# Expert weights in pieces of 2 contraction tiles by 1024 columns, with a PSUM pair for the gate and one for the up projection

## The chip, the cores and the metric

One core of one Trainium2 chip runs the whole program in one launch. The metric is the time of an execution on the device in microseconds (us); several executions are timed and the median counts. All inputs and the output lie in the chip's HBM. The engines named below are TensorE (PE; its weight loads are a row of their own, PEld), VectorE (DVE), ScalarE (ACT), GpSimd (POOL) and SyncE (SP), whose queue issues the loads of the weights.

## The reference, cut to what matters

A decoder trunk of two layers works on 256 tokens of 1024 float32 channels. Each layer has a mixer; then comes a dense SwiGLU on the first layer, and on the second layer a SwiGLU with 8 experts, two of them for each token. The change touches the experts alone:

```python
def moe_swiglu(h, router_w, w1, w3, w2):          # t: [256, 1024]
    logits = jnp.einsum('td,de->te', t, router_w)
    top_vals, top_idx = lax.top_k(logits, TOP_K)  # 2 of 8
    ...
    for e in range(N_EXPERTS):
        a = t @ w1[e]                             # w1, w3: [1024, 2816]
        b = t @ w3[e]
        out = out + gates[:, e:e + 1] * ((jax.nn.silu(a) * b) @ w2[e])   # w2: [2816, 1024]
```

All of it is float32, and the products must be about as exact as float32.

## The kernel before, in words

**Weights.** All weights are streamed once, in loads of 1 MB (`wload`, lines 72 to 89). SP issues the load of a raw tile; ACT then rounds it into a part `whi` (line 86), and DVE subtracts to get the rest, `wlo` (line 88). Each product of the reference becomes three matmuls on such parts: high by high, high by low and low by high. Four raw buffers (more at times: `ring` lends some), three `whi` buffers and two or three `wlo` buffers make up the stream, and the three engines work it off one load after the other.

**Experts.** `moe` gathers each expert's tokens into 128 slots, so that a matmul has 128 rows of slots and up to 512 columns of weights. `slots` then runs over the experts `e` and over pieces of the hidden width of 2816 (`FCH`: five pieces of 512 columns and one of 256). For a piece, `up_proj` multiplies by w1, and again by w3, into the two banks of one PSUM tile `ab` (tag `mm`, two tiles deep). Then ACT takes the Silu of the first bank (line 976) and DVE multiplies by the second (line 977), which gives `sae`. During the next piece `turn` transposes `sae` on PE (line 890) and splits it into `ahe` and `ale`, and `down` multiplies these by w2 into the two PSUM tiles `ye` of the expert, one for each half of the model's width (lines 906 to 908). A piece of 512 takes two loads of w1, two of w3 and two of w2; the last piece takes one of each.

**Scatter.** When an expert is complete, `gated` scales `ye` by the token's gate and splits it into two parts (ACT line 933, DVE line 934): into `tokA` for an even expert, into four tiles `y` of 512 columns for an odd one. Those four lie in buffers lent by the activations' tags, `st01` and `st02` for the first half of the width, `st00` and `st10` for the second. After an odd expert, PE scatters the two experts' rows back to the tokens (`psc`, line 925, PSUM tag `s`, two tiles deep), and DVE adds the result to the residual stream `xt` (line 927). This happens after experts 1, 3 and 5, while the next expert's first piece is under way, and after expert 7, where the final norm and the output follow.

**Order.** A scheduler turns the program into one fixed sequence of instructions for each engine before the run. An engine works its sequence in order; an instruction whose operands or buffers are not free holds up all that stand behind it on that engine.

Of the kernel before, what the change touches and what calls it, by code (L numbers as in the profile page):

```python
# [21 lines left out]
NL = 2            # layers  # L22
# [5 lines left out]
FCH = [(c, min(512, FF - c)) for c in range(0, FF, 512)]  # L28


@with_exitstack
def trunk_kernel(ctx: ExitStack, tc: tile.TileContext, x, w_in, lower_bounds, hgrn_norm_w, conv_w,
# [39 lines left out]
    def wload(src2d, k0, nk, c0, ncol):  # L72
        """rows k0*128.. (nk tiles) x columns c0..c0+ncol, split -> hi, lo [128, nk, ncol]"""
# [100 lines left out]
    # mean squares of the rows of the residual stream, by halves of the width  # L174
# [45 lines left out]
    # ---- the residual stream times a norm's weight, as columns in parts, by halves of the width. The  # L220
    # norm's factor of a token is applied to what is made of them: rstd by token, rbc as a row for all. ----
# [35 lines left out]
    def bounds():  # L257
        """lower bounds of the forget gates: cumulated softmax over the layers, less the first"""
# [33 lines left out]
    # within a block of 4, s <= t  # L292
# [6 lines left out]
    # s in the first, t in the second half of a block of 2m; t of the second halves only  # L299
# [85 lines left out]
    # o = S^T v, normalised per head, gated; token-major  # L385
# [89 lines left out]
    def route_slots(t):  # L475
        """1 + slot of the token within each expert, 0 where not chosen"""
# [6 lines left out]
    # ================= mixer =================  # L483
    def mixer(l):
# [13 lines left out]
        # forget gate, key, query: [key, head, t] in two groups of four heads  # L498
# [21 lines left out]
        # scores, transposed: [s, head, t]  # L520
# [12 lines left out]
        # output gate, token-major: silu(g) * norm weight  # L533
# [10 lines left out]
        # merge gates  # L544
# [12 lines left out]
        # short convolution: [channel, t]  # L557
# [30 lines left out]
        # projections and merge: [d, t]  # L588
# [21 lines left out]
        for g in range(2):  # L610
# [20 lines left out]
            # a token tile after the other, the routing of the first beside the second  # L631
# [25 lines left out]
    # ================= dense SwiGLU =================  # L657
    def dense(l):
# [10 lines left out]
        def down(c0, n, ah, al, w, dh, cs):  # L669
            """columns cs of the weights w, to the half dh of the width"""  # L670
# [11 lines left out]
        for ci, (c0, n) in enumerate(FCH):  # L682
# [15 lines left out]
            else:  # L698
                # the last two: one half of the width after the other
# [22 lines left out]
    # ================= final norm =================  # L722
# [12 lines left out]
    # ================= top-2 expert SwiGLU =================  # L735
    def moe(l):
# [8 lines left out]
        # the factors of a row: of its normalisation, and its gates; by token and by slot  # L745
# [11 lines left out]
        def make_gates():  # L757
            """softmax over the two kept logits"""
# [17 lines left out]
        def late():  # L776
            """what only the scatter needs: the gates, and the largest number of tokens of an expert"""
# [8 lines left out]
        def slots(base):  # L786
            """all experts on their slots base .. base+127"""
# [23 lines left out]
            def gather(e2, first=False):  # L811
# [3 lines left out]
                # one-hot products of the parts: exact  # L815
# [16 lines left out]
                if first:  # L832
                    # the first token tile ahead of the routing of the second
# [40 lines left out]
            def up_proj(src, c0, n, o, xh, xl, es):  # L874
                nh = (KT * n + 2047) // 2048
                per = KT // nh
                for half in range(nh):
                    wh, wl = wload(src, half * per, per, c0, n)
                    for k in range(per):
                        kt = half * per + k  # L880
                        nc.tensor.matmul(o, xh[:, kt, es], wh[:, k, :], start=kt == 0, stop=False)  # L881
                        nc.tensor.matmul(o, xh[:, kt, es], wl[:, k, :], start=False, stop=False)  # L882
                        nc.tensor.matmul(o, xl[:, kt, es], wh[:, k, :], start=False, stop=kt == KT - 1)  # L883

            def turn(e, c0, n, ci, sa, ys):
                """gated activations [slot, f] -> their parts [f, slot]"""
# [4 lines left out]
                ah = big.tile([128, nt, 128], F32R, tag=f"st{ci % 2}1", name="ahe")  # L891
                al = big.tile([128, nt, 128], F32R, tag=f"st{ci % 2}2", name="ale")
# [3 lines left out]
            def down(e, c0, n, ah, al, ys, PT, halves=(0, 1)):  # L896
                nt = n // 128
                for d0, dn in ([(h * 512, 512) for h in halves] if n == 512 else [(0, 1024)]):
                    wh, wl = wload(expert_w2[j, e], c0 // 128, nt, d0, dn)
                    for dh in range(dn // 512):  # L900
                        for k in range(nt):
                            o = ys[d0 // 512 + dh]
                            ds_ = slice(dh * 512, dh * 512 + 512)
                            first = c0 == 0 and k == 0
                            end = c0 + n == FF and k == nt - 1
                            nc.tensor.matmul(o, ah[:, k, :], wh[:, k, ds_], start=first, stop=False)  # L906
                            nc.tensor.matmul(o, ah[:, k, :], wl[:, k, ds_], start=False, stop=False)  # L907
                            nc.tensor.matmul(o, al[:, k, :], wh[:, k, ds_], start=False, stop=end)  # L908
# [27 lines left out]
            pend = None  # L936
# [8 lines left out]
            for e in range(NE):  # L945
# [4 lines left out]
                for ci, (c0, n) in enumerate(FCH):  # L950
# [3 lines left out]
                    ab = psum.tile([128, 2, 512], F32, tag="mm", name="ab")  # L954
                    up_proj(expert_w1[j, e], c0, n, ab[:, 0, 0:n], xh, xl, es)
# [6 lines left out]
                    if base == 0 and e == 0 and ci == 4:  # L962
                        less("tokA")
                    if e == 0 and ci == 3:
                        less("v")
                        PT = hot_t()
                    if pend is not None:
                        pend = turn(*pend)
                    up_proj(expert_w3[j, e], c0, n, ab[:, 1, 0:n], xh, xl, es)
                    if e % 2 == 1 and e + 1 < NE and ci == 2:  # L970
                        less("fc", "qq")
                        nxt = gather(e // 2 + 1)
                    if pend is not None and not final:
                        down(*pend, PT)
                    sa = big.tile([128, n], F32, tag=f"st{ci % 2}0", name="sae")
# [52 lines left out]
```

## Time and profile before

| | before |
|---|---|
| median of 3 runs | 1619.73 us (1618.6 to 1619.83) |
| span of the profiled execution, first to last instruction | 1618.9 us |
| around the span, against the median | 0.8 us |
| mean granted TensorE clock | 0.994 |
| busy: PE, PEld, DVE, ACT | 99%, 88%, 77%, 58% |
| loads of expert weights | 264 of 1 MB, 6.8 us each from issue to landing |

The profile comes from one execution. Its times are in us from the first instruction on; the experts take the stretch from about 827 to 1608. A share of busy time says little by itself: what counts is what an engine waited for when it did not work. The granted clock of TensorE is 1.0 (2.4 GHz) or 0.5 (1.2 GHz).

### The profile page before, as it was taken

The page shows a single profiled execution, that of the slowest core. Times are in us where ns is not written, and L with a number is a line of the kernel's source. Part 1 is how long each engine was busy: PE and PEld are TensorE (multiplying, and loading weights), DVE is VectorE, ACT ScalarE, POOL GpSimd, SP SyncE. Part 2 cuts the span into 40 slices and gives each one's busy share as a digit, 9 for nine tenths or more (in the row PEclk, how much of TensorE's full clock was granted, in tenths as well). Part 3 has the DMA queues.
Part 4 walks back from the last instruction along what each step waited for, and adds up shares of the span by engine and source line. Part 5 has one row for each costly group of instructions (what it writes and reads, how often), then busy time and mean ns, then how long its engine had stood idle before and what let it go on. Part 6 is the DMA issues. An engine that isn't in the chain of part 4 may idle for free.

```text
span 1618.9 us, 23572 instructions
## 1 busy us (share of the span) xinstructions
PE 1594.9 (99%) x9858; PEld 1427.5 (88%) x9858; DVE 1243.7 (77%) x1182; ACT 938.4 (58%) x836; POOL 33.9 (2%) x51
## 2 busy tenths in 40 slices
PE   7999999999999999999999999999999999999997
PEld 7989999999999989999988888888888888888886
DVE  6964785655446965677678898888888888888886
ACT  6434343544335444334467777677776777767775
POOL 2000020000000000010000000000000000000000
PEclk9999999999999999999999999999999999999998
DMA  7544445555654554458568999999999999999992
GB/s 276 183 158 164 149 132 187 180 182 181 201 189 162 177 182 156 157 195 286 171 221 311 352 324 331 337 366 373 339 356 331 364 374 346 365 334 365 373 376 97
DMA packets 215939, 417.06 MB, mean 258 GB/s; under 512 B 6528, under 2 KB 25056, under 8 KB 215824
## 3 DMA queue, kind: packets, MB, share of 16 engines
q1 hardware_dynamic: 215408, 414.25, 73.1%
q8 instruction: 79, 1.29, 0.3%
q0 software_dynamic: 384, 1.21, 0.2%
q14 instruction: 36, 0.29, 0.0%
q10 hardware_dynamic: 32, 0.01, 0.0%
HBM read 414.40 MB, written 1.05 MB: 257 GB/s over the span
## 4 chain that ended last, share of the span: by engine, by line
PE 96%; DVE 2%; ACT 1%; DMA 1%; issue 0%; POOL 0%; SPq 0%; POOLq 0%; DVEq 0%
PE psb L128 11%; PE psb L130 11%; PE psb L132 11%; PE ab L882 10%; PE ab L883 10%; PE ab L881 9%; PE ye L908 5%; PE ye L906 5%; PE ye L907 5%; PE psa L149 2%; PE psa L151 2%; PE psa L150 2%; PE psl L365 1%; PE y L677 1%; PE y L678 1%; PE y L679 1%
## 5 line engine op out<-in xcount | busy, mean ns | idle before, releaser
L86 ACT ACTIVATE whi<-wraw 128x2048 fp32r<-128x2048 f32 (+1 forms) x456 | 760.5, 1679 | 507.8 <-PE psb L130 257.6
L88 DVE TENSOR_TENSOR wlo<-wraw,whi 128x2048 fp32r<-128x2048 f32 (+1 forms) x456 | 900.1, 1993 | 199.7 <-ACT whi L86 93.1
L128 PE MATMUL psb<-hlA,whi 128*128 128x256 f32 x1376 | 393.2, 286 | 2.7 <-ACT hlA L217 2.7
L130 PE MATMUL psb<-hlB,whi 128*128 128x256 f32 x1376 | 390.5, 284 | 0.5 <-DVE hlB L218 0.5
L132 PE MATMUL psb<-hlA,wlo 128*128 128x256 f32 x1376 | 390.3, 284 | 0.0
L128 PEld LDWEIGHTS psb<-hlA,whi 128*128 128x128 f32 x1376 | 264.4, 192 | 3.9 <-ACT hlA L217 3.1
L130 PEld LDWEIGHTS psb<-hlB,whi 128*128 128x128 f32 x1376 | 264.6, 192 | 1.1 <-DVE hlB L218 0.7
L132 PEld LDWEIGHTS psb<-hlA,wlo 128*128 128x128 f32 x1376 | 264.5, 192 | 0.2
L882 PE MATMUL ab<-wlo,bu 128*128 128x512 f32 (+1 forms) x384 | 144.2, 375 | 1.2 <-DVE wlo L88 1.2
L882 PE MATMUL ab<-wlo,fc 128*128 128x512 f32 (+1 forms) x384 | 144.5, 376 | 0.8 <-DVE wlo L88 0.8
L881 PE MATMUL ab<-whi,bu 128*128 128x512 f32 (+1 forms) x384 | 144.2, 376 | 0.0
L881 PE MATMUL ab<-whi,fc 128*128 128x512 f32 (+1 forms) x384 | 143.8, 374 | 0.0
L883 PE MATMUL ab<-whi,kk 128*128 128x512 f32 (+1 forms) x384 | 143.0, 372 | 0.0
L883 PE MATMUL ab<-whi,qq 128*128 128x512 f32 (+1 forms) x384 | 142.9, 372 | 0.0
L907 PE MATMUL ye<-wlo,ahe 128*128 128x512 f32 x352 | 137.7, 391 | 0.7 <-DVE wlo L88 0.7
L908 PE MATMUL ye<-whi,ale 128*128 128x512 f32 x352 | 136.9, 390 | 0.2
L906 PE MATMUL ye<-whi,ahe 128*128 128x512 f32 x352 | 136.6, 390 | 0.0
L882 PEld LDWEIGHTS ab<-wlo,bu 128*128 128x128 f32 x384 | 72.4, 189 | 14.4 <-DVE wlo L88 2.8
L882 PEld LDWEIGHTS ab<-wlo,fc 128*128 128x128 f32 x384 | 72.3, 188 | 14.4 <-DVE wlo L88 2.7
L881 PEld LDWEIGHTS ab<-whi,fc 128*128 128x128 f32 x384 | 72.3, 188 | 12.6
L881 PEld LDWEIGHTS ab<-whi,bu 128*128 128x128 f32 x384 | 72.3, 188 | 12.3
L883 PEld LDWEIGHTS ab<-whi,kk 128*128 128x128 f32 x384 | 72.4, 188 | 12.1
(243 smaller groups left out, 1867.1 us busy)
## 6 DMA issues: line engine op xcount, KB each, us to landing
wraw<-in_expert_w_dram SPq DMA_DIRECT2D x264, 1024.0 KB, 6.8
wraw<-in_w_in_dram SPq DMA_DIRECT2D x72, 1024.0 KB, 5.0
wraw<-in_dense_w_dram SPq DMA_DIRECT2D x33, 1024.0 KB, 5.0
wraw<-in_w_proj_conv_dram SPq DMA_DIRECT2D x8, 1024.0 KB, 5.0
wraw<-in_w_proj_hgrn_dram SPq DMA_DIRECT2D x8, 1024.0 KB, 5.0
wraw<-in_w_out_dram SPq DMA_DIRECT2D x8, 1024.0 KB, 5.0
xt<-in_x_dram SPq DMA_DIRECT2D x2, 512.0 KB, 4.7
out_dram<-bu SPq DMA_DIRECT2D x4, 256.0 KB, 2.9
```

The costliest lines, as they stand in the source:

```text
L86: nc.scalar.activation(hf[:, ks], rf[:, ks], AF.Copy)
L88: nc.vector.tensor_tensor(lf[:, ks], rf[:, ks], hf[:, ks].bitcast(F32), op=ALU.subtract)
L128: nc.tensor.matmul(o, wh[:, k, cs], hh[:, kt, :], start=first, stop=False, skip_group_check=True)
L130: nc.tensor.matmul(o, wh[:, k, cs], hl[:, kt, :], start=False, stop=False, skip_group_check=True)
L132: nc.tensor.matmul(o, wl[:, k, cs], hh[:, kt, :], start=False, stop=last, skip_group_check=True)
L149: nc.tensor.matmul(o, hh[:, kt, ts], wh[:, k, :], start=kt == 0, stop=False)
L881: nc.tensor.matmul(o, xh[:, kt, es], wh[:, k, :], start=kt == 0, stop=False)
L882: nc.tensor.matmul(o, xh[:, kt, es], wl[:, k, :], start=False, stop=False)
L883: nc.tensor.matmul(o, xl[:, kt, es], wh[:, k, :], start=False, stop=kt == KT - 1)
L906: nc.tensor.matmul(o, ah[:, k, :], wh[:, k, ds_], start=first, stop=False)
L907: nc.tensor.matmul(o, ah[:, k, :], wl[:, k, ds_], start=False, stop=False)
L908: nc.tensor.matmul(o, al[:, k, :], wh[:, k, ds_], start=False, stop=end)
```

## The change

The pieces of the experts' hidden width become 1024, 1024 and 768 columns wide (`WIDE`). A load of w1 or w3 then takes 2 contraction tiles of 128 rows by 1024 columns instead of 4 by 512, so that a row of the load is 4096 bytes long instead of 2048 (3072 in the last piece, whose loads have 0.75 MB). A load of w2 takes 2 tiles by the whole width of 1024 instead of 4 by 512. An expert has 35 loads instead of 33, of the same bytes in all. The gate projection gets a PSUM tile `pa` of two banks and the up projection another, `pb`; both come from the tag `mm`, which still has two tiles. Silu, product, transposes and splits work on halves of 512 (or 256) columns as before, now two halves in a row. The matmuls are the same in number and shape.

```diff
+WIDE = [(c, min(1024, FF - c)) for c in range(0, FF, 1024)]
...
             def up_proj(src, c0, n, o, xh, xl, es):
-                nh = (KT * n + 2047) // 2048
-                per = KT // nh
-                for half in range(nh):
-                    wh, wl = wload(src, half * per, per, c0, n)
-                    for k in range(per):
-                        kt = half * per + k
-                        nc.tensor.matmul(o, xh[:, kt, es], wh[:, k, :], start=kt == 0, stop=False)
...
+                for part in range(KT // 2):
+                    wh, wl = wload(src, part * 2, 2, c0, n)
+                    for k in range(2):
+                        kt = part * 2 + k
+                        for p in range(0, n, 512):
+                            ps_ = slice(p, min(p + 512, n))
+                            op = o[:, p // 512, 0:ps_.stop - p]
+                            nc.tensor.matmul(op, xh[:, kt, es], wh[:, k, ps_], start=kt == 0, stop=False)
...
+            def activate(e, c0, n, p, pa, pb):
+                m = min(512, n - p * 512)
+                sa = big.tile([128, m], F32, tag=f"st{p}0", name="sae")
+                nc.scalar.activation(sa, pa[:, p, 0:m], AF.Silu, scale=sc[:, e, 0:1])
+                nc.vector.scalar_tensor_tensor(sa, pb[:, p, 0:m], sc[:, e, 0:1], sa, op0=ALU.mult, op1=ALU.mult)
+                return e, c0 + p * 512, m, p, sa
...
-            def down(e, c0, n, ah, al, ys, PT, halves=(0, 1)):
-                nt = n // 128
-                for d0, dn in ([(h * 512, 512) for h in halves] if n == 512 else [(0, 1024)]):
-                    wh, wl = wload(expert_w2[j, e], c0 // 128, nt, d0, dn)
-                    for dh in range(dn // 512):
-                        for k in range(nt):
-                            o = ys[d0 // 512 + dh]
...
+            def down(e, c0, n, ah, al, ys, PT):
+                for k0 in range(0, n // 128, 2):
+                    wh, wl = wload(expert_w2[j, e], c0 // 128 + k0, 2, 0, 1024)
+                    for k in range(2):
+                        for dh in range(2):
+                            o = ys[dh]
...
-                for ci, (c0, n) in enumerate(FCH):
+                for ci, (c0, n) in enumerate(WIDE):
...
-                    ab = psum.tile([128, 2, 512], F32, tag="mm", name="ab")
-                    up_proj(expert_w1[j, e], c0, n, ab[:, 0, 0:n], xh, xl, es)
+                    pa = psum.tile([128, 2, 512], F32, tag="mm", name="ab")
+                    up_proj(expert_w1[j, e], c0, n, pa, xh, xl, es)
...
+                    pend = [turn(*x) for x in pend]
+                    pb = psum.tile([128, 2, 512], F32, tag="mm", name="ab")
+                    up_proj(expert_w3[j, e], c0, n, pb, xh, xl, es)
...
+                    def acts():
+                        return [activate(e, c0, n, p, pa, pb) + (ys,) for p in range((n + 511) // 512)]
+
+                    if not final:
+                        for x in pend:
+                            down(*x, PT)
+                        pend = acts()
+                        continue
```

`gated` and the scatter are as before, with the same tags for `y`. A second block of the program, for experts with more than 128 tokens, changes alike and is not executed with these inputs. The comments of the file go out, so that lines have other numbers.

The scheduler's order shows what this moves. The number behind a name is that of the tile. The first place is the scatter after expert 1, while the first piece of expert 2 is under way. On PE before, from the last matmul of expert 1's down projection (`ye`) on; `ab_9461` is the next piece of expert 2, with both of its projections:

```order
L908 MATMUL ye_8570<-whi_9410,ale_9369 128x512
L925 MATMUL psc_9430<-tokA_8669,v_8224 128x512 x2
L925 MATMUL psc_9430<-y_9426,v_8224 128x512
L925 MATMUL psc_9436<-tokA_8669,v_8224 128x512 x2
L925 MATMUL psc_9436<-y_9426,v_8224 128x512
L881 MATMUL ab_9461<-whi_9464,fc_8880 128x512
L882 MATMUL ab_9461<-wlo_9465,fc_8880 128x512
L883 MATMUL ab_9461<-whi_9464,qq_8881 128x512
L881 MATMUL ab_9461<-whi_9464,fc_8880 128x512
L882 MATMUL ab_9461<-wlo_9465,fc_8880 128x512
L925 MATMUL psc_9430<-y_9427,v_8224 128x512
L925 MATMUL psc_9436<-y_9427,v_8224 128x512
```

And now, at the same place; `ab_9561` is the gate projection `pa` of the next piece, and takes the buffer of `ab_9307`, the `pa` of the piece before it:

```order
L917 MATMUL ye_8537<-whi_9507,ale_9393 128x512
L934 MATMUL psc_9527<-y_9523,v_8094 128x512
L934 MATMUL psc_9533<-y_9523,v_8094 128x512
L934 MATMUL psc_9527<-y_9524,v_8094 128x512
L934 MATMUL psc_9533<-y_9524,v_8094 128x512
L934 MATMUL psc_9543<-tokA_8754,v_8094 128x512 x2
L934 MATMUL psc_9543<-y_9539,v_8094 128x512
L934 MATMUL psc_9549<-tokA_8754,v_8094 128x512 x2
L934 MATMUL psc_9549<-y_9539,v_8094 128x512
L934 MATMUL psc_9543<-y_9540,v_8094 128x512
L934 MATMUL psc_9549<-y_9540,v_8094 128x512
L883 MATMUL ab_9561<-whi_9564,fc_8929 128x512
```

Before, matmuls of the next piece stand between those of the scatter; now twelve of the scatter stand in one block (two of them are a row with x2), and the next piece's first matmul is behind all of them.

The second place is the same moment on ACT, and then on DVE. On ACT before:

```order
L86 ACTIVATE whi_9464<-wraw_9462 128x2048
L86 ACTIVATE whi_9482<-wraw_9480 128x2048
L933 ACTIVATE y_9426<-ye_8569,sc_7740 128x512
L933 ACTIVATE y_9442<-ye_8570,sc_7740 128x512
L86 ACTIVATE whi_9509<-wraw_9507 128x2048
L976 ACTIVATE sae_9458<-ab_9328,sc_7740 128x512
```

On ACT now:

```order
L942 ACTIVATE y_9523<-ye_8536,sc_7740 128x512
L87 ACTIVATE whi_9582<-wraw_9580 128x2048
L942 ACTIVATE y_9539<-ye_8537,sc_7740 128x512
L87 ACTIVATE whi_9600<-wraw_9598 128x2048
L891 ACTIVATE sae_9555<-ab_9307,sc_7740 128x512
L891 ACTIVATE sae_9558<-ab_9307,sc_7740 128x512
```

A whole `whi` now stands between the two gated halves of the expert, and there are two Silu that both read `ab_9307`. On DVE before:

```order
L88 TENSOR_TENSOR wlo_9483<-wraw_9480,whi_9482 128x2048
L934 SCALAR_TENSOR_TENSOR y_9427<-ye_8569,sc_7740,y_9426 128x512
L934 SCALAR_TENSOR_TENSOR y_9443<-ye_8570,sc_7740,y_9442 128x512
L927 TENSOR_TENSOR xt_76<-xt_76,psc_9430 128x512
L927 TENSOR_TENSOR xt_76<-xt_76,psc_9436 128x512
L88 TENSOR_TENSOR wlo_9510<-wraw_9507,whi_9509 128x2048
```

On DVE now:

```order
L943 SCALAR_TENSOR_TENSOR y_9524<-ye_8536,sc_7740,y_9523 128x512
L89 TENSOR_TENSOR wlo_9583<-wraw_9580,whi_9582 128x2048
L936 TENSOR_TENSOR xt_76<-xt_76,psc_9527 128x512
L936 TENSOR_TENSOR xt_76<-xt_76,psc_9533 128x512
L943 SCALAR_TENSOR_TENSOR y_9540<-ye_8537,sc_7740,y_9539 128x512
L89 TENSOR_TENSOR wlo_9601<-wraw_9598,whi_9600 128x2048
```

There, too, a whole `wlo` has come between the two halves, and the first adds into `xt` stand behind it. At experts 3 and 5 the order now is the same as at expert 1.

The third place is the end, after expert 7. On PE before, from the last `ye` on, all 16 matmuls of the scatter follow:

```order
L908 MATMUL ye_13025<-whi_13758,ale_13729 128x512
L925 MATMUL psc_13784<-tokA_13124,v_8224 128x512 x2
L925 MATMUL psc_13784<-y_13780,v_8224 128x512
L925 MATMUL psc_13784<-y_13781,v_8224 128x512
L925 MATMUL psc_13792<-tokA_13124,v_8224 128x512 x2
...
L925 MATMUL psc_13812<-y_13801,v_8224 128x512
```

Now the eight that read `tokA` stand further ahead, between matmuls of the last piece, and eight follow the last `ye`:

```order
L917 MATMUL ye_13064<-whi_13850,ale_13809 128x512
L934 MATMUL psc_13870<-y_13866,v_8094 128x512
L934 MATMUL psc_13878<-y_13866,v_8094 128x512
L934 MATMUL psc_13890<-y_13886,v_8094 128x512
L934 MATMUL psc_13870<-y_13867,v_8094 128x512
L934 MATMUL psc_13878<-y_13867,v_8094 128x512
L934 MATMUL psc_13898<-y_13886,v_8094 128x512
L934 MATMUL psc_13890<-y_13887,v_8094 128x512
L934 MATMUL psc_13898<-y_13887,v_8094 128x512
```

The transposes of `turn` stand in 31 groups on PE now, in 47 before, since two halves come together.

## Rows read from the trace of the kernel before

**Rows 1.** The page: span, and busy time and instructions of two engines

```profile
span 1618.9 us, 23572 instructions
...
PE 1594.9 (99%) x9858; PEld 1427.5 (88%) x9858; DVE 1243.7 (77%) x1182; ACT 938.4 (58%) x836; POOL 33.9 (2%) x51
```

**Rows 2.** The chain that ended last, shares of the span by engine

```profile
PE 96%; DVE 2%; ACT 1%; DMA 1%; issue 0%; POOL 0%; SPq 0%; POOLq 0%; DVEq 0%
```

**Rows 3.** What PE waited for, 826 to 1605: total us, times, longest

```profile
PE ab L882 <- DVE wlo L88: 2.0, 4, 0.8
PE ye L907 <- DVE wlo L88: 0.7, 2, 0.3
```

**Rows 4.** What SP's queue waited for, 826 to 1605: total us, times, longest

```profile
SPq L76 <- DVE wlo L88: 617.1, 237, 11.7
```

**Rows 5.** DMA issues over the span: count, size, us from issue to landing

```profile
wraw<-in_expert_w_dram SPq DMA_DIRECT2D x264, 1024.0 KB, 6.8
```

**Rows 6.** Groups by form, 826 to 1605: busy us, mean ns; idle before, releasers

```profile
L88 DVE TENSOR_TENSOR wlo<-wraw,whi 128x2048 fp32r<-128x2048 f32 x255 | 579.3, 2289 | 81.7 <-ACT whi L86 80.5 <-DMA wraw<-in_expert_w_dram 0.4
L86 ACT ACTIVATE whi<-wraw 128x2048 fp32r<-128x2048 f32 x255 | 488.6, 1917 | 106.1 <-PE ab L883 72.7 <-PE ye L908 29.8 <-ACT whi L86 2.0
...
L976 ACT ACTIVATE sae<-ab,sc 128x512 f32<-128x512 f32 x40 | 27.6, 691 | 32.4 <-PE ab L883 28.2 <-PE psc L925 4.2
...
L927 DVE TENSOR_TENSOR xt<-xt,psc 128x512 f32<-128x512 f32 x12 | 7.7, 679 | 0.0
...
L934 DVE SCALAR_TENSOR_TENSOR y<-ye,sc,y 128x512 fp32r<-128x512 f32 x7 | 5.1, 746 | 3.0 <-ACT y L933 3.0
```

**Rows 7.** PE's timeline at expert 1's scatter: start, duration in us, operation

```profile
1034.61 0.39 PE L908 MATMUL ye<-whi,ale 128*128 128x512 f32 x1
1034.84 0.62 PE L925 MATMUL psc<-tokA,v 128*128 128x512 f32 x2
...
1037.33 0.68 PE L925 MATMUL psc<-y,v 128*128 128x512 f32 x2
...
1038.77 0.63 PE L925 MATMUL psc<-tokA,v 128*128 128x512 f32 x2
...
1040.63 0.39 PE L881 MATMUL ab<-whi,fc 128*128 128x512 f32 x1
```

**Rows 8.** ACT's timeline there; in brackets the idle time before, and its releaser

```profile
1035.04 0.69 ACT L933 ACTIVATE y<-ye,sc 128x512 fp32r<-128x512 f32 x1 [0.23 <-PE ye L908]
...
1040.60 0.69 ACT L976 ACTIVATE sae<-ab,sc 128x512 f32<-128x512 f32 x1 [3.06 <-PE psc L925]
```

**Rows 9.** PE's timeline at one group of transposes of expert 2

```profile
1060.85 0.60 PE L890 MATMUL pta<-ident,sae 128*128 128x128 f32 x4
1061.20 0.48 PE L881 MATMUL ab<-whi,fc 128*128 128x512 f32 x1
1061.52 0.39 PE L882 MATMUL ab<-wlo,fc 128*128 128x512 f32 x1
```

**Rows 10.** Timelines at the end: PE's scatter, then DVE's adds

```profile
1604.40 0.62 PE L925 MATMUL psc<-tokA,v 128*128 128x512 f32 x2
...
1607.57 0.61 PE L925 MATMUL psc<-y,v 128*128 128x512 f32 x2
...
1605.99 2.01 DVE L927 TENSOR_TENSOR xt<-xt,psc 128x512 f32<-128x512 f32 x3
1608.22 0.69 DVE L927 TENSOR_TENSOR xt<-xt,psc 128x512 f32<-128x512 f32 x1 [0.22 <-PE psc L925]
```

**Rows 11.** Stretches: busy us (count) by engine, PEclk (granted clock), DMA share, GB/s

```profile
9.78:13.19 3.41, 0.53 (x2) 0.19 (x1) 1.42 (x3) 2.08 (x5) 2.65 (x6) 1.00 1.05 390
13.20:16.61 3.41, 3.09 (x14) 3.10 (x15) 3.41 (x9) 3.41 (x9) 0.00 (x0) 0.50 1.06 364
818.74:825.57 6.83, 6.05 (x30) 5.96 (x30) 4.91 (x16) 3.47 (x8) 0.70 (x1) 0.50 0.51 190
1022.00:1050.00 28.00, 28.00 (x128) 22.94 (x127) 25.32 (x19) 19.06 (x14) 0.00 (x0) 1.00 0.91 322
```

More of the change, by code (lines that the diff above doesn't have):

```diff
@@ L874, in up_proj, with turn @@
             def up_proj(src, c0, n, o, xh, xl, es):
-                nh = (KT * n + 2047) // 2048
-                per = KT // nh
-                for half in range(nh):
-                    wh, wl = wload(src, half * per, per, c0, n)
-                    for k in range(per):
-                        kt = half * per + k
-                        nc.tensor.matmul(o, xh[:, kt, es], wh[:, k, :], start=kt == 0, stop=False)
-                        nc.tensor.matmul(o, xh[:, kt, es], wl[:, k, :], start=False, stop=False)
-                        nc.tensor.matmul(o, xl[:, kt, es], wh[:, k, :], start=False, stop=kt == KT - 1)
-            def turn(e, c0, n, ci, sa, ys):
+                for part in range(KT // 2):
[6 more added lines that the diff above has]
+                            nc.tensor.matmul(op, xh[:, kt, es], wh[:, k, ps_], start=kt == 0, stop=False)
+                            nc.tensor.matmul(op, xh[:, kt, es], wl[:, k, ps_], start=False, stop=False)
+                            nc.tensor.matmul(op, xl[:, kt, es], wh[:, k, ps_], start=False, stop=kt == KT - 1)
+            def activate(e, c0, n, p, pa, pb):
[4 more added lines that the diff above has]
+                return e, c0 + p * 512, m, p, sa
+            def turn(e, c0, n, p, sa, ys):
                 nt = n // 128
@@ L890, in turn @@
                     nc.tensor.transpose(ps[:, k, :], sa[:, k * 128:k * 128 + 128], ident)
-                ah = big.tile([128, nt, 128], F32R, tag=f"st{ci % 2}1", name="ahe")
-                al = big.tile([128, nt, 128], F32R, tag=f"st{ci % 2}2", name="ale")
+                ah = big.tile([128, nt, 128], F32R, tag=f"st{p}1", name="ahe")
+                al = big.tile([128, nt, 128], F32R, tag=f"st{p}2", name="ale")
                 split(ps, ah, al)
                 return e, c0, n, ah, al, ys
-            def down(e, c0, n, ah, al, ys, PT, halves=(0, 1)):
-                nt = n // 128
-                for d0, dn in ([(h * 512, 512) for h in halves] if n == 512 else [(0, 1024)]):
-                    wh, wl = wload(expert_w2[j, e], c0 // 128, nt, d0, dn)
-                    for dh in range(dn // 512):
-                        for k in range(nt):
-                            o = ys[d0 // 512 + dh]
-                            ds_ = slice(dh * 512, dh * 512 + 512)
[L904 to L908, printed above, removed]
+            def down(e, c0, n, ah, al, ys, PT):
[4 more added lines that the diff above has]
+                            o = ys[dh]
+                            ds_ = slice(dh * 512, dh * 512 + 512)
+                            first = c0 == 0 and k0 + k == 0
+                            end = c0 + n == FF and k0 + k == n // 128 - 1
+                            nc.tensor.matmul(o, ah[:, k0 + k, :], wh[:, k, ds_], start=first, stop=False)
+                            nc.tensor.matmul(o, ah[:, k0 + k, :], wl[:, k, ds_], start=False, stop=False)
+                            nc.tensor.matmul(o, al[:, k0 + k, :], wh[:, k, ds_], start=False, stop=end)
                 if c0 + n == FF:
@@ L934, in gated @@
                 nc.vector.scalar_tensor_tensor(y[1], src, g, y[0].bitcast(F32), op0=ALU.mult, op1=ALU.subtract)
-            pend = None
+            pend = []
             PT = None
@@ L961, in slots @@
                                 late()
-                    if base == 0 and e == 0 and ci == 4:
+                    if base == 0 and e == 0 and ci == 2:
                         less("tokA")
-                    if e == 0 and ci == 3:
+                    if e == 0 and ci == 1:
                         less("v")
                         PT = hot_t()
[L967 to L970, printed above, removed]
+                    pend = [turn(*x) for x in pend]
+                    pb = psum.tile([128, 2, 512], F32, tag="mm", name="ab")
+                    up_proj(expert_w3[j, e], c0, n, pb, xh, xl, es)
+                    if e % 2 == 1 and e + 1 < NE and ci == 1:
                         less("fc", "qq")
                         nxt = gather(e // 2 + 1)
-                    if pend is not None and not final:
-                        down(*pend, PT)
-                    sa = big.tile([128, n], F32, tag=f"st{ci % 2}0", name="sae")
-                    nc.scalar.activation(sa, ab[:, 0, 0:n], AF.Silu, scale=sc[:, e, 0:1])
-                    nc.vector.scalar_tensor_tensor(sa, ab[:, 1, 0:n], sc[:, e, 0:1], sa, op0=ALU.mult, op1=ALU.mult)
-                    if final:
-                        down(*pend, PT, [0])
-                        end = turn(e, c0, n, ci, sa, ys)
-                        down(*pend, PT, [1])
-                        down(*end, PT)
-                    pend = (e, c0, n, ci, sa, ys)
+                    def acts():
[5 more added lines that the diff above has]
+                        continue
+                    here = acts()
+                    for i, x in enumerate(pend):
+                        down(*x, PT)
+                        here[i] = turn(*here[i])
+                    for x in here:
+                        down(*x, PT)
         slots(0)
```

## The prediction, made before the changed kernel ran

> **What bounds the kernel now.** I read the page first: PE is busy for 1594.9 of 1618.9 us [rows 1], and the chain that ended last runs 96% on PE [rows 2]. So the time is PE's work plus the places where PE stands. Then I looked for those places among the experts. PE waited there 2.0 + 0.7 us, each time for the rest `wlo` from DVE, never for a transfer [rows 3]. In a stretch that holds the scatter after expert 1, PE is busy for all of its 28.00 us, and DVE for 25.32 us, 90% of it [rows 11]. That is what the reader is to see: PE is full, and DVE close behind it has little slack to make good a delay.
>
> The loads come third. SP's queue stood 617.1 us for `wlo` of DVE, which frees the raw buffers [rows 4]; a load takes 6.8 us to land [rows 5], but it is issued when a buffer comes free. The transfers follow the buffers.
>
> Last the scatter after expert 1, in the timeline. The last `ye` matmul starts at 1034.61, the next matmul at 1034.84, so one of 512 columns costs 0.227 us of PE. From 1034.84 to 1040.63 there is hardly a gap, though the scatter must wait for DVE in the middle: the matmuls that use the second parts start at 1037.33, the second half of the width at 1038.77 [rows 7]. Matmuls of the next piece fill the time between. The Silu on ACT started only at 1040.60, held for 3.06 us by the scatter, because its output shares a buffer with `y` [rows 8]. Nothing waited for it: the next piece had an `ab` of its own.
>
> **The change part by part.**
>
> *Matmuls, bytes, DVE and ACT work.* Same counts and shapes, so PE's work stays. 16 loads more of the same bytes cost SP issues only, hidden under its long waits [rows 4]. Taken at 0; ACT and DVE work on as many elements as before.
>
> *Row length of the loads.* Taken at 0, because the queue waits for buffers. If all of the shortage of `wlo` came from transfers, the gain could be no more than the 2.7 us of [rows 3].
>
> *The scatter after experts 1, 3 and 5.* This is the large term. The order now has twelve scatter matmuls in a block, and the next `pa` behind them. It takes the buffer of the earlier `pa`, so both of that piece's Silu must be done; the Silu write to `st00` and `st10`, in which `y_9539` and `y_9540` lie until the block's end. I step through it from D, the moment when the last `ye` of the odd expert has been issued (1034.84 in the rows). A reader of PSUM starts 0.43 us after the last matmul's start: 1034.61 to 1035.04 [rows 7, 8].
>
> 1. ACT: `y_9523` needs the fourth `ye` from the end, which starts at D - 4 x 0.227 = D - 0.91; it runs from D - 0.48 for 0.69 us [rows 8] to D + 0.2. The `whi_9582` behind it takes 1.92 us [rows 6] to D + 2.1; `y_9539` then to D + 2.8.
> 2. DVE: `y_9524`, 0.75 us [rows 6], from D + 0.2 to D + 0.95. Then `wlo_9583`, which needs `whi_9582`: D + 2.1 + 2.29 = D + 4.4. The two adds behind it, 0.68 each, end at D + 5.1 and D + 5.75; `y_9540` at D + 6.5.
> 3. PE: four matmuls, done by D + 1.5. The next, of `psc_9543`, needs a PSUM tile of `s`, which the first add frees at D + 5.1. So **PE stands for 3.6 us**. Six matmuls follow, until about D + 6.5, then the two that read `y_9540`, done at D + 7.0.
> 4. ACT: the first Silu runs when `y_9539` has been read, from about D + 6.6 for 0.69 [rows 6] to D + 7.3; the second needs the end of the block, D + 7.2, and ends at D + 7.9.
> 5. PE: the next piece starts at D + 8.0. In between it did 12 x 0.227 = 2.7 us of work, so 5.3 us are lost; before, about 0.1 [rows 7].
>
> Three times 5.2 are **15.5 us**. The low bound is 0: it holds if an engine finds its operands otherwise than the order says. For the high bound every step would come one `wlo` (2.29) later: 22 us. I take 15.5, since each duration has its own row. What is behind the next piece does not come late as well: four of its loads take PE 10.9 us, in which DVE makes up what it did not do. That the lost time is not won back later follows from [rows 1]: PE has no idle time to win it from.
>
> The Trainium skill speaks against the change here. Its main page "Trainium Kernel Development and Optimization", Best Practices, says that a bubble that recurs can mean that SBUF or PSUM ran out. The rule gives no time; by it the sign is that of my sum.
>
> *The clock.* In the stretch 9.78 to 13.19 PE worked for 0.53 us and stood for 2.9, and the granted clock was 0.5 in the next 3.41 us, in which 14 matmuls were done. At 818.74 it was 0.5 for 6.83 us, with 30 matmuls [rows 11]. The new gap of 3.6 us is longer than those 2.9, so I expect a fall. At half speed 3.41 us lose at most 1.7 us of work; some of that falls where PE waits anyway (D + 7.0 to D + 8.0). Bounds: 0, and 6.83 / 2 = 3.4 us per gap. I take 1.0, nearer the first row: **3.0 us** for the three.
>
> The Trainium skill's page "TensorE: Matmul & The Clock Gate", section "Why this matters for your kernels", says that idle gaps between bursts of matmuls bring back the lower clock. Its rule agrees with the row at 13.20; no run here shows yet whether these three gaps suffice.
>
> *The end.* Before, 16 matmuls follow the last `ye`, from 1604.40 to about 1608.0, beside `gated` and the adds, and the last add waits 0.22 us for PE [rows 10]. Now eight of them come ahead of the last `ye`, which is then 8 x 0.227 = 1.8 us later. The chain behind it, by the same durations: second half gated at about 1.7 after that point, four adds of 0.68 up to 4.3 after; before, the last add ended at 1608.91, 4.5 after. So the end is 1.6 to 2.0 us later; **1.8 us**.
>
> *Transposes.* The matmul after a group of transposes is followed 0.32 us later by the next instead of 0.227 [rows 9]. With 16 groups fewer, 16 x 0.09 = **1.4 us** are gained; at the least 0.
>
> *Other waits.* The 2.7 us of [rows 3] may go or come back at other places, as the `wlo` now fall elsewhere: 0, between -3 and +3.
>
> The sum against the profiled execution: 1618.9 + 15.5 + 3.0 + 1.8 - 1.4 = 1637.8 us of span, and with the 0.8 us around it **1638.6 us**; I say 1638. The median of before is 0.8 us over the span too.
>
> **The rivals.**
>
> *The scatter stays hidden.* If the scatter's wait were filled (the block's PSUM tiles coming free early, as they did at 1037 before), only the end and the transposes change: 1619.7 + 1.8 - 1.4 = 1620 us. For it speaks that before, the same dependences cost nothing [rows 7]; against it that the matmuls which filled them now stand behind the block.
>
> *Only part of the stall.* If DVE's add is not held by `wlo_9583`, because `whi_9582` is ready sooner, the first gap of 3.6 us falls and only Silu's wait remains, its 0.69 twice and the time to the first reading, some 1.7 us a time: 1619.7 + 5 + 0.4 = 1625 us.
>
> *Faster: longer rows help.* The place is the stream of loads of w1 to w3. The stretch 1022 to 1050 moves 322 GB/s at a DMA share of 0.91 [rows 11], so the transfers are not far from full. If they decide when `wlo` is ready, DVE would have its tile sooner, the idle 81.7 us of DVE ahead of `wlo` [rows 6] would shrink, and the waits of [rows 3] and some of those a scatter causes would go. It decides only if the scatter's stall does not come; then 1619.7 - 2.7 - 1.4 + 1.8 = 1617 us, and at the most 1606 us: 24.0 us of the span are without PE work [rows 1], 10.7 of them lie behind the last matmul (1608.2 to 1618.9 [rows 1, 10]), and all the other 13.3 would be gone. Against it: of the 81.7 us, DMA has 0.4.
>
> By the Trainium skill, "DMA: Bandwidth & Descriptors", section "Why small descriptors are slow (HBM only)", a packet has a fixed overhead of some 3 cycles on beats of 32 bytes; an estimate from that is 67 against 131 cycles for twice the bytes, 2.2% less transfer time. A stream waiting for buffers would show none of it.
>
> *Clock twice as long.* If each gap brings the 6.83 us of [rows 11], it is 3 x 2.4 us more: 1645 us.
>
> **How the numbers follow.** Chances: the forecast, with a clock fall of nothing to 1.5 us a gap (1634 to 1641), 0.60; part of the stall (1623 to 1633) 0.13; the longer clock fall or more (1641 to 1650) 0.09; hidden scatter (1617 to 1622) 0.12; faster by the rows' length 0.06. A run tells a difference of about 0.2% (3.2 us) from none. Slower by more than that: 0.60 + 0.13 + 0.09 = 0.82; the same 0.12, faster 0.06. The range from 1621 to 1646 leaves out the faster case, half of the hidden one and a third of the longest, 0.06 + 0.06 + 0.03 = 0.15.
>
> **What the changed profile would show.** Right: three gaps of PE, at the scatters after experts 1, 3 and 5, each some 3.6 us before the third pair of `psc` and then about 1 us before the first matmul into `ab`, the latter released by the Silu; a granted clock of 0.5 behind them; the end 14.5 us after the last `ye`, as now, with that `ye` 1.8 us later by itself; SP still waiting for `wlo`. Wrong: if PE shows no gap there, the order's dependences are not what I read; if the gap is there and the total is not, PE had slack elsewhere; if PE waits for `wlo` all along the experts, DVE or ACT has become the bound, which I priced at 0 to 3; if SP's queue waits less and PE's small waits vanish, the rows' length counted.

## The result, and the profile after

The changed kernel takes 1648.73 us (median of 4 runs, 1648.31 to 1649.06), beside 1619.78 us for the kernel before: slower by a factor of 1.0178, 95% interval 1.0164 to 1.0193. That is 29.0 us; forecast were 18, and the range ended at 1646. The direction and the places were right, the size was not.

The page after, span and busy time, answers to [rows 1]:

```profile
span 1646.5 us, 23673 instructions
...
PE 1609.1 (98%) x9858; PEld 1433.7 (87%) x9858; DVE 1244.6 (76%) x1193; ACT 940.6 (57%) x848; POOL 33.9 (2%) x51
```

DVE and ACT did as much as before. PE has as many matmuls and is busy 14 us longer (1609.1 against 1594.9), so some of them went slower.

Stretches of the changed kernel answer to [rows 11] (length, then busy us and count for PE, PEld, DVE, ACT and POOL, PEclk, DMA share, GB/s). The first is the expert stage from the first up projection to behind the last `ye`, the others are those behind the three scatters:

```profile
824.86:1631.89 807.03, 791.69 (x3742) 655.91 (x3741) 680.41 (x464) 572.73 (x424) 0.00 (x0) 0.98 0.89 328
...
1046.42:1056.66 10.24, 8.56 (x19) 6.28 (x20) 6.90 (x9) 1.68 (x3) 0.00 (x0) 0.50 0.66 222
1251.21:1261.45 10.24, 8.31 (x19) 6.07 (x20) 7.15 (x9) 1.93 (x3) 0.00 (x0) 0.50 0.62 210
1456.02:1466.26 10.24, 8.19 (x18) 5.95 (x19) 7.27 (x9) 2.05 (x3) 0.00 (x0) 0.50 0.59 207
```

The same stage of the kernel before, in the same view:

```profile
826.62:1604.40 777.78, 774.95 (x3735) 646.85 (x3734) 679.63 (x454) 570.78 (x412) 0.00 (x0) 1.00 0.96 341
```

All of the loss, 807.03 - 777.78 = 29.25 us, lies in this stage. (The two spans differ by 27.6 us only: ahead of the experts this execution spent 3.41 us at a granted clock of 0.5, from 817.72 on, where the one before spent 6.83 [rows 11]. So stages are compared below, and not spans.) Three times the granted clock is 0.5 for 10.24 us, in which PE gets 18 or 19 matmuls done.

What PE waited for among the experts (total us, times, longest), beside [rows 3]:

```profile
PE psc L934 <- DVE xt L936: 9.6, 3, 3.2
PE ab L884 <- DVE wlo L89: 2.9, 3, 1.3
PE ab L883 <- ACT sae L891: 2.3, 3, 0.8
```

And PE's timeline at the scatter after expert 1, the place of [rows 7] (start, duration, operation, in brackets the idle time before it and its releaser):

```profile
1042.11 0.39 PE L917 MATMUL ye<-whi,ale 128*128 128x512 f32 x1
1042.60 1.52 PE L934 MATMUL psc<-y,v 128*128 128x512 f32 x4
1047.32 1.22 PE L934 MATMUL psc<-tokA,v 128*128 128x512 f32 x2 [3.20 <-DVE xt L936]
1048.34 0.63 PE L934 MATMUL psc<-y,v 128*128 128x512 f32 x1
...
1049.62 1.48 PE L934 MATMUL psc<-y,v 128*128 128x512 f32 x3
1051.88 0.80 PE L883 MATMUL ab<-whi,fc 128*128 128x512 f32 x1 [0.78 <-ACT sae L891]
1052.47 0.63 PE L884 MATMUL ab<-wlo,fc 128*128 128x512 f32 x1
1052.90 0.63 PE L885 MATMUL ab<-whi,qq 128*128 128x512 f32 x1
```

Two waits, one for DVE's add and one for ACT's Silu. Behind the first, matmuls start 0.43 us apart (1052.47 to 1052.90) where they took 0.227 before: the lower clock. ACT and DVE at the same place:

```profile
1041.85 0.69 ACT L942 ACTIVATE y<-ye,sc 128x512 fp32r<-128x512 f32 x1 [2.84 <-PE ye L917]
1042.44 1.90 ACT L87 ACTIVATE whi<-wraw 128x2048 fp32r<-128x2048 f32 x1
1044.24 0.68 ACT L942 ACTIVATE y<-ye,sc 128x512 fp32r<-128x512 f32 x1
...
1050.29 0.69 ACT L891 ACTIVATE sae<-ab,sc 128x512 f32<-128x512 f32 x1 [3.57 <-PE psc L934]
1051.14 0.69 ACT L891 ACTIVATE sae<-ab,sc 128x512 f32<-128x512 f32 x1 [0.16 <-PE psc L934]
...
1044.38 2.29 DVE L89 TENSOR_TENSOR wlo<-wraw,whi 128x2048 fp32r<-128x2048 f32 x1 [1.05 <-ACT whi L87]
1046.59 1.28 DVE L936 TENSOR_TENSOR xt<-xt,psc 128x512 f32<-128x512 f32 x2
```

The adds wait behind a whole `wlo`, and that behind a whole `whi`. Both Silu wait for the scatter, as the Silu did in [rows 8]; but now the next piece waits for them.

SP's queue, [rows 4], still waits for `wlo`:

```profile
SPq L77 <- DVE wlo L89: 630.3, 255, 10.2
```

### The profile page after: what moved, and what is told of

It is laid out like the page before. It is cut to its first block, busy times and chain, and to the rows that moved or that the text cites. A ratio compares the mean times of both kernels' runs of the same rounds, so it can differ in the third digit from the quotient of the medians.

```text
span 1646.5 us, 23673 instructions
## 1 busy us (share of the span) xinstructions
PE 1609.1 (98%) x9858; PEld 1433.7 (87%) x9858; DVE 1244.6 (76%) x1193; ACT 940.6 (57%) x848; POOL 33.9 (2%) x51
## 5 line engine op out<-in xcount | busy, mean ns | idle before, releaser
L87 ACT ACTIVATE whi<-wraw 128x2048 fp32r<-128x2048 f32 (+2 forms) x467 | 763.1, 1646 | 562.3 <-PE psb L131 257.3
L89 DVE TENSOR_TENSOR wlo<-wraw,whi 128x2048 fp32r<-128x2048 f32 (+2 forms) x467 | 901.9, 1950 | 220.1 <-ACT whi L87 113.2
L915 PE MATMUL ye<-whi,ahe 128*128 128x512 f32 x352 | 128.8, 390 | 0.0
L885 PEld LDWEIGHTS ab<-whi,qq 128*128 128x128 f32 x384 | 73.2, 190 | 12.8
```

What stands on the lines that cost most here:

```text
L87: nc.scalar.activation(hf[:, ks], rf[:, ks], AF.Copy)
L89: nc.vector.tensor_tensor(lf[:, ks], rf[:, ks], hf[:, ks].bitcast(F32), op=ALU.subtract)
L885: nc.tensor.matmul(op, xl[:, kt, es], wh[:, k, ps_], start=False, stop=kt == KT - 1)
L915: nc.tensor.matmul(o, ah[:, k0 + k, :], wh[:, k, ds_], start=first, stop=False)
```

## Theories and experiments

Theory S: the scatter's block of matmuls holds the Silu, the Silu holds the PSUM tile of the next `pa`, and the gap brings the clock down. Rival L: the new loads, or their order against DVE's work, make the stage slower; a fix of the scatter would then help little. Within S it is open how much the clock takes, and beside S what the longer rows do. Stages below are measured in one profiled execution each, from the first up projection to behind the last `ye`.

**e1: free tags for `y`.** On the changed kernel:

```diff
-                               for tag in (("st01", "st02"), ("st00", "st10"))[dh]]
+                               for tag in (("st01", "st02"), ("st11", "st12"))[dh]]
```

> The change with one line altered: the second half of an odd expert's y lies in the buffers of st11 and st12 instead of st00 and st10, so that no Silu writes where the scatter still reads. Nothing is left out. Theory S (the scatter's block of matmuls holds the Silu, the Silu holds the PSUM tile of the next gate projection, and the gap brings the clock down): the three gaps of PE go, the granted clock stays at 1.0 through the experts, and the time is about 1619 us (1617 to 1622), 29 less than with the change. Rival L (the new loads, or their order against DVE's work, make the expert stage slower): the gaps stay or turn up elsewhere, 1640 us or more.

Measured: 1627.49 us (5 runs), ratio to the kernel before 1.0047, 1.0033 to 1.006. The clock stays at 1.0 through the stage. The timeline at the same scatter has matmuls of the next piece between those of the scatter again:

```profile
1043.98 0.39 PE L883 MATMUL ab<-whi,fc 128*128 128x512 f32 x1
1044.25 0.73 PE L934 MATMUL psc<-y,v 128*128 128x512 f32 x2
1044.82 0.39 PE L884 MATMUL ab<-wlo,fc 128*128 128x512 f32 x1
```

The stage, and what PE waits for in it:

```profile
825.67:1610.59 784.92, 779.76 (x3742) 647.80 (x3741) 678.51 (x464) 571.35 (x425) 0.00 (x0) 1.00 0.91 337
```

```profile
PE ab L884 <- DVE wlo L89: 3.6, 6, 1.3
PE ye L916 <- DVE wlo L89: 1.6, 3, 0.5
```

Two tags give back 21.2 of the 29.0 us, with the same loads. Theory S holds for that part and rival L falls for it. But 1619 was expected: 8 us are left, and PE waits for DVE's `wlo` nine times and 5.2 us where it waited six times and 2.7 us in [rows 3].

**e2: PE kept busy in the gap.** On the changed kernel, idle PE time is filled with repeats:

```diff
+                            for again in range(4 if e < NE - 1 and dh == 0 and t == 1 else 1):
...
-                                                     start=i == q == 0, stop=i == q == 1)
+                                                         start=i == q == 0, stop=i == q == 1)
```

> The change, with the four matmuls of one scatter tile (the first half of the width, second token tile) done four times over after experts 1, 3 and 5: 12 matmuls more at each, on PE alone, where it stood for 3.2 us; the result of the tile is the same. Theory S with the clock as its larger part: the wait for the adds and the Silu stays about as long (5 us a time), but the granted clock stays at 1.0 or falls for a shorter time, so some 1634 us (1631 to 1640). Rival (the loss is the wait alone, and the clock does not matter because PE waits meanwhile): 1648 us or more.

Measured: 1641.29 us (4 runs), ratio 1.0127, 1.0111 to 1.0142. PE's timeline:

```profile
1043.37 0.39 PE L917 MATMUL ye<-whi,ale 128*128 128x512 f32 x1
...
1048.59 0.73 PE L935 MATMUL psc<-tokA,v 128*128 128x512 f32 x2 [0.46 <-DVE xt L937]
...
1052.16 0.50 PE L883 MATMUL ab<-whi,fc 128*128 128x512 f32 x1 [1.13 <-ACT sae L891]
```

The stage:

```profile
826.11:1623.86 797.75, 789.39 (x3778) 655.09 (x3777) 680.11 (x464) 572.25 (x424) 0.00 (x0) 1.00 0.90 332
```

The clock is 1.0 all through. From D (the last `ye` plus 0.227) the second half of the scatter starts at D + 4.99, in the changed kernel at D + 4.98: the same wait for DVE, filled or not. The next piece starts at D + 8.56 instead of D + 9.54. So the 36 added matmuls make the kernel 7.4 us faster, and the stages differ by 807.03 - 797.75 = 9.3 us: **3.1 us a scatter are the clock's.** It came out 7 us above the expected time, and just outside its range. A stall takes 5.8 us (8.56 less 12 x 0.227) instead of the 5 expected, 2.5 us in all; the 1.6 us of the end (e9) were left out; and the kernel before took 0.8 us more beside these runs (1620.58). The last 2 us are open. The late `wlo` of e1 are not the reason, for PE waits for `wlo` here about as in [rows 3]:

```profile
PE ab L884 <- DVE wlo L89: 2.9, 3, 1.3
```

**e3: `whi` and `wlo` behind the gates and adds.** On the changed kernel, tags unchanged:

```diff
-                        gated(ys[dh], e, odd)
+                        ga = gated(ys[dh], e, odd)
...
+                    if e < NE - 1:
+                        ring["order"] = [(None, None), (ga, d0x)]
```

(`d0x` is the last add of the first half.)

> The change, with the split of the second load after each scatter put in order behind the gated second half (ACT) and behind the first two adds (DVE). Nothing is left out, the tags are those of the change. Theory S: the adds no longer stand behind a wlo, so that PE's gap of 3.2 us falls to about 0.9; the Silu is still held, and PE stands some 2 us more before the next piece; without a fall of the clock 3 x 3.4 us over the time before, 1630 us (1626 to 1635), with one 1645. Rival L: no change, 1648 us.

Measured: 1630.03 us (4 runs), ratio 1.0057, 1.0042 to 1.0073. What PE waits for:

```profile
PE ab L883 <- ACT sae L891: 3.8, 3, 1.3
PE ab L884 <- DVE wlo L89: 2.9, 3, 1.3
PE psc L934 <- DVE xt L936: 1.6, 3, 0.6
```

The wait for the adds falls from 3.2 to 0.6 at most, that for the Silu stays, and at 0.6 and 1.3 us the clock does not fall (1.0 in the stage). So it was the large split ahead of the adds that made the long gap, and the long gap that cost the clock.

**e6: old loads.** On e1, all expert loads in the shapes of the kernel before (`up_proj` goes over the halves `p`, then over loads of `2048 // m` tiles by `m` columns; `down` loads as before); pieces and PSUM pairs as changed.

```diff
-                for part in range(KT // 2):
-                    wh, wl = wload(src, part * 2, 2, c0, n)
+                for p in range(0, n, 512):
+                    m = min(512, n - p)
+                    nk = 2048 // m
...
+                        wh, wl = wload(src, k0, nk, c0 + p, m)
```

> As e1 (free tags for y), with all expert loads in the old shapes: 4 tiles by 512 columns (2048 byte rows), the last 256 columns in 8 tiles; the wide pieces and the pair of PSUM tiles stay. Theory S with row length at nothing: the same as e1 within 3 us. Rival (longer rows shorten the transfers and with them PE's small waits): slower than e1 by 3 to 10 us.

Measured: 1624.02 us (11 runs), ratio 1.0022, 1.0013 to 1.0031; the stage is 781.59 us. Shorter rows are 3.5 us faster here: against the sign of the rival, and half a us more than Theory S allowed. The edit changes the order of the matmuls along with the loads; e11 below tells the two apart.

**e7 and e5: one kind of load each.** e7 has only the w2 loads of the old kind, e5 only those of w1 and w3; both on e1, with the edits of e6.

> As e1, but the loads of w2 in the old shape and order (4 tiles by 512 columns, one half of the width after the other); w1 and w3 stay at 2 tiles by 1024. Nothing is left out. e1 took 1627.5 us, e6 (all loads old) 1624.0; PE's small waits in the expert stage were 19.4 and 14.9 us. Theory U (the new shape of w1 and w3 makes the waits): as e1, 1626 to 1628. Theory W (that of w2 makes them): as e6, 1623 to 1625.

> As e1, but the loads of w1 and w3 in the old shape (4 tiles by 512 columns, 8 by 256 at the end); w2 stays at 2 tiles by 1024. Nothing is left out. Theory U: as e6, 1623 to 1625. Theory W: as e1, 1626 to 1628.

Measured: e7 1625.89 (6 runs), 1.003, 1.0018 to 1.0042, stage 783.54; e5 1627.28 (6 runs), 1.0034, 1.0022 to 1.0047, stage 784.34. Against e1's 784.92, w2 back gives 1.4 us, w1 and w3 back 0.6, both (e6) 3.3. But the profiled execution of e5 begins its stage at the lower clock, and none of the others above does:

```profile
826.82:829.91 3.09, 3.09 (x8) 2.46 (x9) 2.91 (x6) 0.00 (x0) 0.00 (x0) 0.50 0.27 42
```

Its first seven matmuls took 3.12 us (826.82 to 829.94), those of e1 1.68 (825.67 to 827.35). Less these 1.44 us, e5's stage is 782.9, and w1 and w3 back give 2.0 us. With the 1.4 of w2 that is the 3.3 of both. Neither theory holds alone, and the times do not put the two kernels in order: the intervals of their ratios overlap almost wholly.

**e8: the kernel before with w2 in rows of 4096 bytes.**

```diff
-                for d0, dn in ([(h * 512, 512) for h in halves] if n == 512 else [(0, 1024)]):
-                    wh, wl = wload(expert_w2[j, e], c0 // 128, nt, d0, dn)
+                for k0 in [2 * h for h in halves] if n == 512 else [0]:
+                    wh, wl = wload(expert_w2[j, e], c0 // 128 + k0, 2, 0, 1024)
```

> The kernel before, with its w2 loads of whole pieces as 2 tiles by 1024 (rows of 4096 bytes instead of 2048) and nothing else changed: 80 of its 264 expert loads. If the row length counts: up to 3 us faster. If it does not, because the queue waits for buffers: the same within 2 us, but for the end of the program, where both halves of the width now end together: 0 to 2 us slower.

Measured: 1624.38 us (11 runs), ratio 1.0021, 1.0012 to 1.003: 3.4 us or so slower by the ratio (1.9 to 4.9), where the second case allowed 2. The stage grew by 2.3 us, to 780.12:

```profile
PE ab L882 <- DVE wlo L88: 3.8, 6, 0.8
PE ye L907 <- DVE ale L51: 1.4, 2, 0.7
```

Again it is DVE that is late, not a transfer. But the row length is not all that this edit changes, as the expectation has it: the loops over `k` and `dh` change places too, so that the two halves of `ye` end 3 matmuls apart instead of 6. By e11 below, that order alone is worth 2.8 us in e1, as much as was lost here. So e8 does not tell what longer rows are worth.

**e9: the last scatter behind the last `ye`.** On e1:

```diff
+                            with behind(last["ye"] if e == NE - 1 else None):
```

> As e1, with the scatter after expert 7 put behind the last ye on PE, so that the eight matmuls that read tokA come after it again. Nothing is left out. If they cost their time ahead of the last ye and nothing behind it: 1.4 us less than e1 (1.0 to 1.8), 1626. Rival: no difference, the end hangs on gating and adds.

Measured: 1625.96 us (5 runs), ratio 1.0036, 1.0023 to 1.005; 1.5 us less than e1. The stage is 783.30, 1.6 less. By the stage the rival falls; the times alone overlap in their intervals.

**e11: the halves of the last w2 load one after the other.** On e1:

```diff
-                    for k in range(2):
-                        for dh in range(2):
+                    for k, dh in ([(0, 0), (1, 0), (0, 1), (1, 1)] if c0 + n == FF and k0 + 2 == n // 128 else
+                                  [(0, 0), (0, 1), (1, 0), (1, 1)]):
```

> As e1, but in the last w2 load of each expert one half of the width comes after the other, so that the first half is complete 6 matmuls (1.36 us) ahead of the second instead of 3, as in the kernel before. Loads as with the change, nothing left out. If PE's small waits come from gating both halves at the same moment, they fall and the stretch from the first up projection to behind the last ye shortens from e1's 784.9 us to about 783.5, as in e7: 1626 us. If the shape of the loads makes them: no difference, 1627.5 us.

Measured: 1624.38 us (11 runs), ratio 1.0022, 1.0012 to 1.0031. The stage:

```profile
825.80:1607.91 782.11, 778.93 (x3742) 648.17 (x3742) 678.93 (x465) 571.37 (x424) 0.00 (x0) 1.00 0.92 339
```

It is 2.8 us shorter than e1's with the same loads, twice the 1.4 expected. PE's waits for `wlo` in the up projections fall from e1's 3.6 us, six times, to

```profile
PE ab L884 <- DVE wlo L89: 1.6, 3, 0.8
```

So 2.8 of the 7.1 us by which e1's stage was longer than before came from gating both halves of an expert at nearly the same moment. And here the row length can be read: e6 has the old loads and the same distance between the halves, and took 1624.02 us with a stage of 781.59, where e11 with rows twice as long took 1624.38 and 782.11. That is no difference that these runs can tell, in whichever direction (e6 has its other matmuls in another order as well). e7, too, has the halves 6 matmuls apart, so that its 1.4 us are not the shape of the w2 loads alone.

**e10 and e13: the edits together.** e10 is e6 with the edit of e9; e13 is the change with those of e1, e9 and e11.

> As e6 (wide pieces and PSUM pairs, free tags, all loads in the old shapes), with the last scatter put behind the last ye. Nothing is left out. e6 took 1624.0, e9 was 1.5 us under e1: 1622.5 us (1621 to 1624), 2 us above the kernel before. What then is left would be the wide pieces' own: two Silu, products and splits in a row.

> The change with the three edits of e1, e9 and e11 together: other tags for y, the last scatter behind the last ye, and one half of the width after the other in each expert's last w2 load. All loads as with the change, nothing left out. If the edits add up: e11's 1624.4 us less e9's 1.5, 1622.9 us (1621.5 to 1624), still 2 us or so above the kernel before, for rows twice as long. Rival: the last scatter gains nothing where the first half is complete earlier, 1624.4.

Measured: e10 1623.23 us (11 runs), 1.0018, 1.0009 to 1.0027; e13 1622.72 us (11 runs), 1.0016, 1.0007 to 1.0025. e10 gained 0.8 us on e6 where 1.5 were expected, less than these runs can tell. e13 came out as expected, with a stage of 780.7 us; its time alone does not shut out the rival, as its interval reaches to 1624.7. It is the best version with the new loads. It and e10, alike but for the loads and their order, are 0.5 us apart, again no difference. No version was faster than the kernel before.

## Why the prediction was right in its places and wrong in its size

The loss of the stage, 29.25 us, taken apart by the kernels: 9.3 the clock (changed kernel less e2), 797.75 - 784.92 = 12.8 the stall without it (e2 less e1), 1.6 the eight matmuls at the end (e1 less e9), and the rest of e1 over the kernel before, 5.5. Term by term beside the prediction, in the changed kernel itself: clock 9.3 where 3.0 were forecast, stall 17.2 (5.84 each, less the 0.1 of before) for 15.5, end 1.6 for 1.8, and what is left, transposes and other waits, 1.1 for -1.4. The two lists differ because the stall and e1's small waits do not add up (see 3).

1. **What bounds the kernel**: right. PE is the bound; in the stage it is busy for 791.69 of 807.03 us.
2. **Row length at 0**: right. SP waits for buffers as before, and rows twice as long show no gain where the order is alike (e11 beside e6, e13 beside e10). The faster rival is out.
3. **The stall**: right in every step and nearly in size. `y` on ACT was forecast for D - 0.48 and came at D - 0.49; the second half of the scatter for D + 5.1, came at D + 4.98; the next piece at D + 8.0, and at full clock (e2) it came at D + 8.56, at all three scatters. The 5.8 us so lost are 0.5 more than forecast. (3 x 5.2 is 15.6, not 15.5.) Beside e1, though, a scatter cost 4.3 net, 12.8 for the three. I had said that nothing would be won back. In part it was. Counted in the traces from start to start, beyond the 0.227 us of a matmul, the delays of over 0.02 us that begin at a matmul reading `wlo` come to 5.9 us in the kernel before, 9.9 in e1 and 5.5 in e2. So e1 has 4.4 us of small delays that e2 has not, nearly all of the 4.7 between three times 5.84 and 12.8; that fits DVE catching up while PE stands. e1 and e3 show both links, the tag and the split ahead of the adds.
4. **The clock: this is the step that failed.** I took 1.0 us a gap, "nearer the first row", from a fall of 3.41 us of which part would fall into waiting. The fall lasted 10.24 us, longer than either row of before, and cost 3.1 us a gap, 9.3 instead of 3.0. That is 6.3 of the 10 us that the forecast was short. The upper bound of 3.4 us a gap covered it, but I gave the longer fall 0.09. By itself it would have made 1645 us, still inside the range; the stall (1.7) and the sixth point (2.5) took the time out of it. That the clock would fall at all was right.
5. **The end**: right, 1.6 us of 1.8.
6. **Other waits at 0, transposes at -1.4**: wrong; 1.1 us were lost there in the changed kernel, and 5.5 show once the stall is gone (e1). The transposes gain nothing. In [rows 9] the second matmul behind a group of four starts 0.35 + 0.32 us after the group does, so two groups take 1.34 us. A group of eight in e1:

```profile
892.89 1.04 PE L900 MATMUL pta<-ident,sae 128*128 128x128 f32 x8
893.68 0.48 PE L883 MATMUL ab<-whi,bu 128*128 128x512 f32 x1
894.00 0.39 PE L884 MATMUL ab<-wlo,bu 128*128 128x512 f32 x1
```

That is 0.79 + 0.32 us, and 0.23 for the matmul that makes up the count: 1.34 us as well. I had counted the 0.09 us behind each group, and not that the last transpose of a group is followed sooner than one within it. Of the 5.5 us, e11 shows where 2.8 come from: the two halves of `ye` now end 3 matmuls apart, and gating both falls on ACT and DVE at once, ahead of the splits that PE needs next. I saw that order (a `whi` between the gates) only for its effect on the scatter. The last 2.7 us are late `wlo` too for the larger part (the delays of point 3 are 7.7 us in e11, 1.8 more than before); what in the wide pieces makes them late is open. e5's 2.0 us say that the w1 and w3 loads, or the order that comes with them, have a part in it, and e10 that the old loads do not remove it all.

## What to carry to other kernels

Where a matmul stream is full, a coarser piece costs by what it bunches: look in the scheduled order for the place where the side work that once lay between two pieces comes in one block, and for the tile whose buffer the next piece needs. See too how far apart two results end that the same engines must take away: another order of the last matmuls of an expert gave back 2.8 us. A tag that was free to lend is free only for the old piece size; moving `y` to two other tags gave back 21 of 29 us. And price a gap of PE by what the clock does behind it, not by its length alone: filling the gap with repeated work was worth 7.4 us.

## What the runs showed of the hardware

PE stood for 3.2 us in a full stream of matmuls (1044.12 to 1047.32). The granted clock fell to 0.5 at 1046.42, inside this gap, stayed there for 10.24 us and rose at 1056.66, when PE had been at the next piece for 4.8 us; likewise at the other two scatters. The kernel before had 3.41 and 6.83 us of it behind its own thin stretches [rows 11]. In e3 PE stood 0.6 and then 1.3 us within 4 us, and the clock stayed at 1.0. The Trainium skill, "TensorE: Matmul & The Clock Gate", section "Why this matters for your kernels", warns of idle gaps between bursts of matmuls; these rows agree. A fall cost 3.1 us here (e2).
